# A hybrid decoder layer on one core: background steps divided by engine, more of the work turned into steps, one table for Exp and Ln

## The chip, the core and the metric

The kernel runs on one core of one Trainium2 chip. A core has a matrix engine (TensorE, PE in the profile; its weight loads are PEld), a vector engine (VectorE, DVE), an activation engine (ScalarE, ACT), GpSimd (POOL) and SyncE (SP), which only issues transfers here. Each engine works through its own instructions in their order and waits for the others by semaphores. The metric is the device time of one execution in microseconds (us), lower is better. The median of three runs before the change is 1818.29 us.

## The reference

One layer of a decoder, batch 1, 256 positions, width 2048, everything in float32:

```
h  = rmsnorm(x);  proj = h @ w_in          # 2048 columns in, 15376 out
A: gated delta rule:  q, k, v = silu(causal conv of 4 taps);  beta = sigmoid(..)
   logdecay = -exp(a_log) * softplus(.. + dt_bias);  triangular solve by chunks
   o_a = head_rmsnorm(o) * gain * silu(z_a)
B: HGRN2:  log f = logaddexp(log lb, log1p(-lb) + log_sigmoid(f));  k = -expm1(log f)
   gated linear recurrence;  o_b = head_rmsnorm(o) * gain * silu(z_b)
C: attention of 4 heads from each position into 256 memory tokens
merged = sum over A, B, C of sigmoid(gate) * (o @ w_br)
x = x + rmsnorm(merged @ w_out)
x = x + rmsnorm(relu(rmsnorm(x) @ w1)^2 @ w2)      # 8192 wide
```

All of it has to be computed; the output is x, 256 by 2048.

## The kernel before

**Units.** The large products are cut into units of 512 output columns. A unit goes through 2048 rows of weights in eight groups of 256 rows. A group's weights come in by one transfer (`w`, four buffers), ACT rounds them to `wh` (L153), DVE forms the rest `wl = w - wh` (L154), and PE multiplies by both parts: L185 to L187 in a plain unit (`unit`), L202 for the wide products and L204 for the narrow ones in a joined unit (`unit_joined`). A joined unit's result is put together from PSUM into an SBUF tile `sum` by ACT (L239) and DVE (L240). The PSUM accumulators of the units (`mm`) have two buffers, the background's banks four. Most SBUF tiles come from one pool of 25 slots (`g4`).

**Background.** Everything that isn't a unit is written as a generator: `gen_c` (attention), `gen_a` (delta rule, one for each half of the heads), `gen_b` (HGRN2, one for each half), `gen_merge` and others. A piece of a generator between two `yield`s is a *step*. The list `bg` holds the generators, and they run one after the other. After each group of a unit `tick` adds a rate to a credit and runs as many steps as the credit has whole numbers (half a group of a joined unit adds half). The rates R1 to R4 hold for the four phases: the eight units of A's projections with attention behind them; branch C (four pairs of a gate unit and a unit of `w_br`, 48 ticks); the eight units of B's projections; branch A (48 ticks), and what follows. Ahead of branch A a loop runs steps until both halves of `gen_a` are done, behind it `drain` runs whatever is left.

**Order.** The code fixes for each instruction what it depends on. A planner with its own cost table then sets the order on each engine, roughly by the order in the code among the instructions that it takes to be ready. `pin` keeps an instruction behind the one that was written before it on the same engine.

**What stands outside the steps.** `ab_unit` (beta, the log decays `ld` and their sums, with the `te` products at L660 and L661) runs as a whole ahead of A's units. `conv_evac` (the convolution: per head one ACT and three DVE operations, and one Silu), `z_evac` (Silu and a product with the gain) and `f_evac` (the forget gate: Abs, Exp, Ln, two DVE operations, four Exps) run as a whole behind their units.

**Tables.** ACT holds one set of functions at a time. The loads are put in automatically: for a function that the loaded set lacks, the first set that has it. The set found first for Exp has no Ln, so Exp, Ln, Exp takes three loads.

Lines that the prediction speaks of: L843 (X) and L849 (its transposes XT); L805 to L807 (`sse`, the power on POOL, `rq`); L790 (U and AQ); L956 (the gates' Sigmoid); L1028 and L1030 (`join_halves`); L1037 to L1051 (Exps and products of a level); L1058 (`pa` products); L1064 to L1070 (predicated copies into AT).

Of the kernel before, what the change touches and what calls it, by code (L numbers as in the profile page):

```python
# [13 lines left out]
AF = mybir.ActivationFunctionType  # L14
# [22 lines left out]
R1, R2, R3, R4 = 0.5, 1.0, 0.8, 0.8  # L37
# [3 lines left out]
def tile_trunk(ctx: ExitStack, tc, a):  # L41
# [71 lines left out]


# [328 lines left out]
    def gen_start():  # L443
# [41 lines left out]
        A.activation(e, e, AF.Exp)  # L485
# [5 lines left out]
        A.activation(lbl1, lb, AF.Ln, bias=1.0, scale=-1.0)  # L491
        c1, c2 = small("c1", 8), small("c2", 8)
        V.tensor_scalar(out=c1, in0=lb, scalar1=TINY, scalar2=None, op0=ALU.max)
        A.activation(c1, c1, AF.Ln)
# [137 lines left out]
    def ab_unit():  # L632
        wst = g4("wabs", (P, KT, 32), F32R)
        A.copy(wst[:, :, 0:16], wab)
        V.tensor_tensor(out=wst[:, :, 16:32], in0=wab, in1=wst.bitcast(F32)[:, :, 0:16], op=ALU.subtract)
        ps = bank("ab")
        for kt in range(KT):
            for i, x_ in enumerate(hact(kt)):
                T.matmul(ps[0:32, 0:S], wst[:, kt, :], x_, start=kt == 0 and i == 0, stop=kt == KT - 1 and i == 1)
        abT = g4("abT", (P, S))  # L640
        V.tensor_copy(abT[0:32, :], ps[0:32, 0:S])
        pt = bank("abt")
        for t in range(NT):
            T.transpose(pt[:, t * 32:(t + 1) * 32], abT[0:32, t * P:(t + 1) * P], ident[0:32, 0:32])
        ab2 = small("ab2", 64).rearrange("p (t c) -> p t c", t=NT)
        V.tensor_copy(ab2, pt[:, 0:64].rearrange("p (t c) -> p t c", t=NT))
        pv = small("abs", 32).rearrange("p (t c) -> p t c", t=NT)
        V.tensor_tensor(out=pv, in0=ab2[:, :, 0:16], in1=ab2[:, :, 16:32], op=ALU.add)
        A.activation(beta, pv[:, :, 0:8], AF.Sigmoid)
        xx, ax = small("xx"), small("ax")  # L650
        x3 = xx.rearrange("p (t h) -> p t h", t=NT)
        V.tensor_tensor(out=x3, in0=pv[:, :, 8:16], in1=dtb.unsqueeze(1).to_broadcast([P, NT, 8]), op=ALU.add)
        A.activation(ax, xx, AF.Abs)
        A.activation(ax, ax, AF.Exp, scale=-1.0)
        A.activation(ax, ax, AF.Ln, bias=1.0)
        V.scalar_tensor_tensor(out=xx, in0=xx, scalar=0.0, in1=ax, op0=ALU.max, op1=ALU.add)
        V.scalar_tensor_tensor(out=ld, in0=x3, scalar=-1.0, in1=alog.unsqueeze(1).to_broadcast([P, NT, 8]),
                               op0=ALU.mult, op1=ALU.mult)
        pd = bank("te")
        T.matmul(pd[:, 0:8], mgt, ld[:, 0, :], start=True, stop=True)  # L660
        T.matmul(pd[:, 8:16], caus, ld[:, 1, :], start=True, stop=True)  # L661
        A.activation(t0e, pd[:, 0:8], AF.Exp)
        A.activation(e1e, pd[:, 8:16], AF.Exp)
        V.tensor_copy(ldh, ld)
        V.tensor_tensor(out=ldl, in0=ld, in1=ldh.bitcast(F32), op=ALU.subtract)

    ab_unit()
# [6 lines left out]
    def conv_evac(ps, which, hg):  # L674
        cv = g4("cv4", (P, 4, S))
        for h in range(4):
            ct = which * 8 + hg * 4 + h
            o, p = cv[:, h, :], ps[:, h, :]
            A.activation(o, p, AF.Copy, scale=ccol[:, 72 + ct:73 + ct])
            for d in (1, 2, 3):  # L680
                tap = 3 - d
                V.scalar_tensor_tensor(out=o[:, d:], in0=p[:, 0:S - d],
                                       scalar=ccol[:, tap * 24 + ct:tap * 24 + ct + 1],
                                       in1=o[:, d:], op0=ALU.mult, op1=ALU.add)
        A.activation(cv, cv, AF.Silu)
        return cv

    def z_evac(ps, g):
        z = g4("z", (P, NT * 4, P))
        A.activation(z, ps.rearrange("p (b d) -> p b d", d=P), AF.Silu)  # L690
        V.tensor_tensor(out=z, in0=z, in1=g.unsqueeze(1).to_broadcast([P, NT * 4, P]), op=ALU.mult)
        return z
# [32 lines left out]
    def gen_a(hg, kc, qc, vc, z):  # L725
# [50 lines left out]
        for t in range(NT):  # L776
            pks = [gram(t, t, hp) for hp in range(2)]
            for h in range(4):
# [7 lines left out]
                                   op0=ALU.mult, op1=ALU.mult)  # L786
            for h in range(4):
                b = t * 4 + h
                for w, dst in ((0, U), (1, AQ)):
                    V.scalar_tensor_tensor(out=dst[:, b, :], in0=pks[h // 2][:, (h % 2) * S + w * P:(h % 2) * S + w * P + P],  # L790
                                           scalar=cneg[:, b:b + 1], in1=d2[t][:, h, w, :],
                                           op0=ALU.mult, op1=ALU.mult)
            yield
# [4 lines left out]
        for k in range(NB):  # L798
            sl = slice(k * BL, (k + 1) * BL)
            G.dma_start(scr[k].rearrange("b c m -> c b m"), U[sl, :, sl])  # L800
# [4 lines left out]
        V.tensor_scalar(out=sse, in0=sse, scalar1=EPS, scalar2=None, op0=ALU.add)  # L805
        G.tensor_tensor(out=nr, in0=sse, in1=pexp, op=ALU.pow)
        V.tensor_scalar(out=rq, in0=nr[:, 8:16], scalar1=DKS, scalar2=None, op0=ALU.mult)  # L807
# [28 lines left out]
        for c in range(BL - 2, -1, -1):  # L836
# [4 lines left out]
            if c % 2 == 0:  # L841
                yield
        V.tensor_tensor(out=X.rearrange("p b (k c) -> p b k c", c=BL), in0=Xc.unsqueeze(2).to_broadcast([P, 8, NB, BL]),  # L843
                        in1=mblk.rearrange("p (k c) -> p k c", c=BL).unsqueeze(1).to_broadcast([P, 8, NB, BL]), op=ALU.mult)
        yield
# [75 lines left out]
        yield  # L921
        yield from head_out(o, z, rq, oa, hg)

    for hg in range(2):
        kc = conv_evac(unit_joined(hboth, w_in, OFF_AK + 512 * hg), 1, hg)
        qc = conv_evac(unit_joined(hboth, w_in, OFF_AQ + 512 * hg), 0, hg)
        vc = conv_evac(unit_joined(hboth, w_in, OFF_AV + 512 * hg), 2, hg)
        z = z_evac(unit(hact, KT, w_in, OFF_AZ + 512 * hg), gna)
        bg.append(gen_a(hg, kc, qc, vc, z))
# [21 lines left out]
    def branch(gi, o, w_br):  # L951
        oact = act_of(o)
        for j in range(4):
            ps = unit(hact, KT, w_in, OFF_G + gi * D + 512 * j)
            sg = g4("sg", (P, NT, 512))
            A.activation(sg, ps.rearrange("p (t n) -> p t n", t=NT), AF.Sigmoid)  # L956
# [13 lines left out]
    def f_evac(ps, hg):  # L970
        p3 = ps
        e = g4("fe", (P, 4, S))
        A.activation(e, p3, AF.Abs)
        A.activation(e, e, AF.Exp, scale=-1.0)
        A.activation(e, e, AF.Ln, bias=1.0)
        t, g = g4("ft", (P, 4, S)), g4("fg", (P, 4, S))
        V.scalar_tensor_tensor(out=t, in0=p3, scalar=0.0, in1=e, op0=ALU.max, op1=ALU.add)
        V.scalar_tensor_tensor(out=g, in0=p3, scalar=0.0, in1=e, op0=ALU.min, op1=ALU.subtract)
        for h in range(4):
            c = hg * 4 + h  # L980
            A.activation(t[:, h, :], t[:, h, :], AF.Exp, scale=-1.0, bias=lbl1[:, c:c + 1])
        return t, g

    def gen_b(hg, k, g, q, v, z):
# [39 lines left out]
        def join_halves(s):  # L1024

            n = 1024 // (2 * s)
            pl = PP.rearrange("p h (n t s) -> p (h n) t s", t=2, s=s)
            V.tensor_tensor(out=hv(R, s, False), in0=hv(R, s, False), in1=pl[:, :, 1, s - 1:s].to_broadcast([P, n, s]),  # L1028
                            op=ALU.add)
            V.tensor_tensor(out=hv(PP, s, True), in0=hv(PP, s, True), in1=pl[:, :, 0, s - 1:s].to_broadcast([P, n, s]),  # L1030
                            op=ALU.add)
# [3 lines left out]
        for li, s in enumerate((1, 4, 16)):  # L1035
# [4 lines left out]
            V.tensor_tensor(out=seg(0, s), in0=seg(0, s), in1=bv(q, s), op=ALU.mult)  # L1040
            if s == 1:
                kp = k
            else:
                kp = kps[li % 2]
                A.activation(kp, R, AF.Exp)
                V.tensor_tensor(out=kp, in0=kp, in1=k, op=ALU.mult)
            join_halves(s)
            yield
            A.activation(seg(1, 2 * s), bv(PP, 2 * s), AF.Exp)
            V.tensor_tensor(out=seg(1, 2 * s), in0=seg(1, 2 * s), in1=bv(q, 2 * s), op=ALU.mult)  # L1050
            V.tensor_tensor(out=seg(2, 2 * s), in0=seg(1, 2 * s), in1=e1.unsqueeze(3).to_broadcast([P, 8, nb, 2 * s]),  # L1051
                            op=ALU.mult)
            join_halves(2 * s)
            yield
            pas = [bank("pa") for _ in range(4)]
            for h in range(4):
                for t in range(NT):
                    T.matmul(pas[h][:, t * 192:t * 192 + 192], kp[:, h, t * P:(t + 1) * P], qp[:, h * 2 + t, 0:192],  # L1058
                             start=True, stop=True)
            first = mT[s].bitcast(I32).rearrange("p (n r s) -> p n r s", r=4, s=s)[:, :, 1, :]  # L1060
# [11 lines left out]
            yield  # L1072

        A.activation(seg(0, 64), bv(PP, 64), AF.Exp)
        V.tensor_tensor(out=seg(0, 64), in0=seg(0, 64), in1=bv(q, 64), op=ALU.mult)
        kp = kps[1]
        A.activation(hv(kp, 64, False), hv(R, 64, False), AF.Exp)
        V.tensor_tensor(out=hv(kp, 64, False), in0=hv(kp, 64, False), in1=hv(k, 64, False), op=ALU.mult)
        join_halves(64)
        yield  # L1080
        pa = bank("pa")
# [272 lines left out]
```

## Time and profile before

| | us |
|---|---|
| median of three runs (1817.17 to 1819.19) | 1818.29 |
| the profiled execution | 1818.59 |
| its span, first to last instruction | 1816.9 |
| PE busy in the span | 1797.2 |
| DVE, ACT, POOL busy | 1133.6, 914.6, 42.9 |
| mean granted PE clock | 0.997 |

A row of a group or a wait gives the line and the engine, the tile written and the tiles read, and then times in us; a row of the order of time begins with the start from the span's beginning and the duration. A duration runs from start to end; the next instruction may start before that end. A stretch's row gives its length and each engine's busy time, then PE's granted clock (1.00 is full).

### The profile page before, as it was taken

How to read it: one execution, taken by the hardware profiler on the slowest of the kernel's cores; microseconds unless marked ns; L12 is line 12 of the kernel's file. 1: busy time of each engine (PE TensorE's matmuls, PEld its weight loads, DVE VectorE, ACT ScalarE, POOL GpSimd, SP SyncE). 2: the span in 40 equal slices, each digit the busy share in tenths (PEclk: the TensorE clock that was granted, in tenths of full speed). 3: DMA queues.
4: the chain of work that ended last, by engine and by line, in shares of the span. 5: the costliest groups of instructions: out<-in, count | busy, mean ns of one | idle time of the engine just before them, and what ended most of it. 6: DMA issues, size and time to landing. Idle time of an engine off the chain costs nothing.

```text
span 1816.9 us, 23842 instructions
## 1 busy us (share of the span) xinstructions
PE 1797.2 (99%) x9241; PEld 1533.5 (84%) x9241; DVE 1133.6 (62%) x1518; ACT 914.6 (50%) x1158; POOL 42.9 (2%) x68
## 2 busy tenths in 40 slices
PE   9999999999999989999999999999999999999998
PEld 8888888888888878888888888888888888888886
DVE  6865768746655685874555557655655565656556
ACT  6745666545546655654444445544444444444433
POOL 1100000200200000000000000000000000000000
PEclk9999999999999999999999999999999999999999
DMA  8675554855654636556766665566666676666664
GB/s 271 197 201 153 172 164 150 221 156 150 183 162 140 185 105 197 151 158 191 218 186 188 210 218 176 181 196 193 190 191 192 193 213 191 192 193 190 185 198 138
DMA packets 174946, 333.40 MB, mean 184 GB/s; under 512 B 13144, under 2 KB 14832, under 8 KB 174576
## 3 DMA queue, kind: packets, MB, share of 16 engines
q1 hardware_dynamic: 169280, 325.10, 59.6%
q10 hardware_dynamic: 4528, 4.54, 0.8%
q0 software_dynamic: 1024, 2.23, 0.7%
q8 instruction: 72, 1.18, 0.3%
q14 instruction: 42, 0.34, 0.1%
HBM read 329.60 MB, written 2.23 MB: 183 GB/s over the span
## 4 chain that ended last, share of the span: by engine, by line
PE 91%; DVE 5%; ACT 2%; issue 1%; DMA 1%; POOL 0%; DVEq 0%; POOLq 0%; ACTq 0%
PE mm L202 21%; PE mm L185 17%; PE mm L186 17%; PE mm L187 17%; PE mm L204 11%; DVE wl L154 1%; ACT wh L153 1%; DMA x<-in_x 0%; PE pzt L874 0%; PE pw L869 0%; PE pa L1058 0%; DVE AT L1067 0%; DVE bR L1028 0%; DMA w<-in_w_kv_mem 0%; DMA alog<-in_a_log 0%
## 5 line engine op out<-in xcount | busy, mean ns | idle before, releaser
L154 DVE TENSOR_TENSOR wl<-w,wh 128x1024 fp32r<-128x1024 f32 x600 | 730.3, 1222 | 533.8 <-ACT wh L153 532.9
L153 ACT CAST wh<-w 128x1024 fp32r<-128x1024 f32 x600 | 630.2, 1052 | 703.7 <-PE mm L187 444.7
L202 PE MATMUL mm<-h2h,wh 128*128 128x512 f32 x960 | 230.7, 391 | 0.0
L185 PE MATMUL mm<-wh,hh 128*128 128x512 f32 x576 | 226.4, 393 | 0.0
L186 PE MATMUL mm<-wl,hh 128*128 128x512 f32 x576 | 224.8, 390 | 1.2 <-DVE wl L154 1.2
L187 PE MATMUL mm<-wh,hh 128*128 128x512 f32 x576 | 224.8, 390 | 0.0
L202 PEld LDWEIGHTS mm<-h2h,wh 128*128 128x128 f32 x960 | 176.3, 188 | 34.0
L186 PE MATMUL mm<-wl,mh 128*128 128x512 f32 x512 | 199.2, 389 | 0.0
L185 PE MATMUL mm<-wh,mh 128*128 128x512 f32 x512 | 199.2, 389 | 0.0
L187 PE MATMUL mm<-wh,ml 128*128 128x512 f32 x512 | 199.2, 389 | 0.0
L202 PE MATMUL mm<-hh,wh 128*128 128x512 f32 x768 | 194.3, 395 | 1.0 <-DVE sum L240 1.0
L202 PEld LDWEIGHTS mm<-hh,wh 128*128 128x128 f32 x768 | 138.7, 189 | 26.1 <-DVE sum L240 1.4
L186 PEld LDWEIGHTS mm<-wl,hh 128*128 128x128 f32 x576 | 108.2, 188 | 23.2 <-DVE wl L154 1.7
L187 PEld LDWEIGHTS mm<-wh,hh 128*128 128x128 f32 x576 | 108.2, 188 | 22.5
L204 PEld LDWEIGHTS mm<-h2h,wl 128*128 128x128 f32 x960 | 123.1, 191 | 4.7
L185 PEld LDWEIGHTS mm<-wh,hh 128*128 128x128 f32 x576 | 108.2, 188 | 21.5
L204 PE MATMUL mm<-h2h,wl 128*128 128x256 f32 x960 | 124.5, 283 | 0.0
L185 PEld LDWEIGHTS mm<-wh,mh 128*128 128x128 f32 x512 | 96.1, 188 | 20.0
L186 PEld LDWEIGHTS mm<-wl,mh 128*128 128x128 f32 x512 | 96.1, 188 | 20.0
L187 PEld LDWEIGHTS mm<-wh,ml 128*128 128x128 f32 x512 | 96.1, 188 | 19.8
L204 PEld LDWEIGHTS mm<-hh,wl 128*128 128x128 f32 x768 | 103.1, 192 | 11.0 <-DVE wl L154 5.1
L204 PE MATMUL mm<-hh,wl 128*128 128x256 f32 x768 | 107.1, 285 | 4.3 <-DVE wl L154 4.3
(394 smaller groups left out, 1919.7 us busy)
## 6 DMA issues: line engine op xcount, KB each, us to landing
w<-in_w_in SPq DMA_DIRECT2D x240, 512.0 KB, 3.8
w<-in_w_mlp_in SPq DMA_DIRECT2D x128, 512.0 KB, 4.2
w<-in_w_mlp_out SPq DMA_DIRECT2D x128, 512.0 KB, 4.3
w<-in_w_out SPq DMA_DIRECT2D x32, 512.0 KB, 4.3
w<-in_w_kv_mem SPq DMA_DIRECT2D x30, 512.0 KB, 5.0
w<-in_w_br_c SPq DMA_DIRECT2D x16, 512.0 KB, 4.4
w<-in_w_br_a SPq DMA_DIRECT2D x16, 512.0 KB, 4.4
w<-in_w_br_b SPq DMA_DIRECT2D x16, 512.0 KB, 3.8
```

The lines of the kernel that those rows point to most:

```text
L153: q(A.copy(wh[:, js, 0:width], w[:, js, 0:width]))
L154: q(V.tensor_tensor(out=wl[:, js, 0:width], in0=w[:, js, 0:width], in1=wh.bitcast(F32)[:, js, 0:width], op=ALU.subtract))
L185: T.matmul(o, st, wh[:, j, :], start=kt == 0, stop=False)
L186: T.matmul(o, st, wl[:, j, :], start=False, stop=False)
L187: T.matmul(o, sl, wh[:, j, :], start=False, stop=kt == nk - 1)
L202: T.matmul(ps[c], wh[:, j, c * P:(c + 1) * P], both[j], start=k0 + j == 0, stop=end)
L204: T.matmul(ps[c][:, 0:S], wl[:, j, c * P:(c + 1) * P], both[j][:, 0:S], start=False, stop=end)
```

## The change

Six things are edited.

1. `ab_unit` becomes the generator `gen_ab` of six steps, first in the background. Its Exp follows a loaded set that has Exp and Ln both, as everywhere below where `exp_ln_table` stands: an Abs on ACT, kept behind the last Silu or Sigmoid, then the load of that set, pinned.
2. `conv_evac`, `f_evac` and the DVE part of `z_evac` become generators of five, four and one steps. `ahead_of_all` puts them at the head of `bg`, behind earlier ones of their kind.
3. `gen_a` has 44 steps instead of 41: the U and AQ copies are cut in two for each half of the positions, and an empty step stands before XT. The addition to `sse` and the power stand ahead of the second half's U and AQ, pinned; `rq` moves to the end; the first scratch DMAs are pinned.
4. `gen_b` has 42 steps instead of 20: Exps, products, the halves of `join_halves`, the `pa` products and the predicated copies (two heads at a time) are steps of their own.
5. The first Exp and Ln at the start (lower bounds) go by the joint set too.
6. The rates go from 0.5, 1.0, 0.8, 0.8 to 1.1, 1.0, 1.0, 1.2.

The core of the diff ("..." for lines left out):

```diff
-R1, R2, R3, R4 = 0.5, 1.0, 0.8, 0.8
+R1, R2, R3, R4 = 1.1, 1.0, 1.0, 1.2
...
+    def own_table(ins):
+        other_table[0] = ins.ins
+        return ins
+
+    def exp_ln_table(out, in_):
+        with tc.issue_after(other_table[0]) if other_table[0] is not None else nullcontext():
+            A.activation(out, in_, AF.Abs)
+        pin(A.preload_act_table_set("natural_log_exp_and_others"))
...
+    def ahead_of_all(gen):
+        while first_of and first_of[0] not in bg:
+            first_of.pop(0)
+        bg.insert(len(first_of), gen)
+        first_of.append(gen)
...
-    def ab_unit():
+    def gen_ab():
...
-        A.activation(ax, xx, AF.Abs)
-        A.activation(ax, ax, AF.Exp, scale=-1.0)
-        A.activation(ax, ax, AF.Ln, bias=1.0)
+        exp_ln_table(ax, xx)
+        pin(A.activation(ax, ax, AF.Exp, scale=-1.0))
+        pin(A.activation(ax, ax, AF.Ln, bias=1.0))
...
+        yield
+        yield
         pd = bank("te")
...
-    ab_unit()
+    bg.append(gen_ab())
     bg.append(gen_c())
...
-    def conv_evac(ps, which, hg):
+    def conv(ps, which, hg):
+
         cv = g4("cv4", (P, 4, S))
+        def steps():
+            for h in range(4):
...
+                yield
+            own_table(A.activation(cv, cv, AF.Silu))
+            yield
+        ahead_of_all(steps())
         return cv
...
+            if t == 1:
+                pin(V.tensor_scalar(out=sse, in0=sse, scalar1=EPS, scalar2=None, op0=ALU.add))
+                pin(G.tensor_tensor(out=nr, in0=sse, in1=pexp, op=ALU.pow))
             for h in range(4):
...
-            yield
+                if h % 2 == 1:
+                    yield
...
-            G.dma_start(scr[k].rearrange("b c m -> c b m"), U[sl, :, sl])
+            pin(G.dma_start(scr[k].rearrange("b c m -> c b m"), U[sl, :, sl]))
...
-        V.tensor_scalar(out=sse, in0=sse, scalar1=EPS, scalar2=None, op0=ALU.add)
-        G.tensor_tensor(out=nr, in0=sse, in1=pexp, op=ALU.pow)
-        V.tensor_scalar(out=rq, in0=nr[:, 8:16], scalar1=DKS, scalar2=None, op0=ALU.mult)
...
         yield
+        yield
         for t in range(NT):
             pt = bank("XT")
...
+        pin(V.tensor_scalar(out=rq, in0=nr[:, 8:16], scalar1=DKS, scalar2=None, op0=ALU.mult))
         yield from head_out(o, z, rq, oa, hg)
...
+    def forget(ps, hg):
+        t, g = g4("ft", (P, 4, S)), g4("fg", (P, 4, S))
+        def steps():
+            e = g4("fe", (P, 4, S))
+            exp_ln_table(e, ps)
+            pin(A.activation(e, e, AF.Exp, scale=-1.0))
+            pin(A.activation(e, e, AF.Ln, bias=1.0))
+            yield
+            yield
+            V.scalar_tensor_tensor(out=t, in0=ps, scalar=0.0, in1=e, op0=ALU.max, op1=ALU.add)
+            yield
+            for h in range(4):
+                c = hg * 4 + h
+                A.activation(t[:, h, :], t[:, h, :], AF.Exp, scale=-1.0, bias=lbl1[:, c:c + 1])
+            V.scalar_tensor_tensor(out=g, in0=ps, scalar=0.0, in1=e, op0=ALU.min, op1=ALU.subtract)
+            yield
+        ahead_of_all(steps())
         return t, g
...
-            V.tensor_tensor(out=seg(0, s), in0=seg(0, s), in1=bv(q, s), op=ALU.mult)
             if s == 1:
                 kp = k
             else:
                 kp = kps[li % 2]
                 A.activation(kp, R, AF.Exp)
-                V.tensor_tensor(out=kp, in0=kp, in1=k, op=ALU.mult)
-            join_halves(s)
-            yield
+            yield
+            for step in join_halves(s):
+                yield
             A.activation(seg(1, 2 * s), bv(PP, 2 * s), AF.Exp)
+            V.tensor_tensor(out=seg(0, s), in0=seg(0, s), in1=bv(q, s), op=ALU.mult)
+            yield
...
-            join_halves(2 * s)
-            yield
+            yield
+            if s > 1:
+                V.tensor_tensor(out=kp, in0=kp, in1=k, op=ALU.mult)
+                yield
             pas = [bank("pa") for _ in range(4)]
...
+            yield
             first = mT[s].bitcast(I32).rearrange("p (n r s) -> p n r s", r=4, s=s)[:, :, 1, :]
...
-            yield
+                if h % 2 == 1:
+                    yield
+            for step in join_halves(2 * s):
+                yield
```

More of the change, by code (lines that the diff above doesn't have):

```diff
@@ L1 @@
-from contextlib import ExitStack
+from contextlib import ExitStack, nullcontext
 import numpy as np
@@ L112, in tile_trunk @@
     A.copy(warm, warm)
+    other_table = [None]
+    def own_table(ins):
[5 more added lines that the diff above has]
+        pin(A.preload_act_table_set("natural_log_exp_and_others"))
     bg = []
@@ L127, in drain @@
             pump(1)
+    first_of = []
+    def ahead_of_all(gen):
[3 more added lines that the diff above has]
+        first_of.append(gen)
     rate, credit = [1.0], [0.0]
@@ L484, in gen_start @@
         V.tensor_tensor(out=e, in0=raw, in1=raw, op=ALU.subtract)
-        A.activation(e, e, AF.Exp)
+        exp_ln_table(e, e)
+        pin(A.activation(e, e, AF.Exp))
         re = small("re", 8)
@@ L490, in gen_start @@
         V.tensor_tensor(out=lb, in0=pr, in1=pr, op=ALU.subtract)
-        A.activation(lbl1, lb, AF.Ln, bias=1.0, scale=-1.0)
+        pin(A.activation(lbl1, lb, AF.Ln, bias=1.0, scale=-1.0))
         c1, c2 = small("c1", 8), small("c2", 8)
         V.tensor_scalar(out=c1, in0=lb, scalar1=TINY, scalar2=None, op0=ALU.max)
-        A.activation(c1, c1, AF.Ln)
+        pin(A.activation(c1, c1, AF.Ln))
         V.tensor_scalar(out=c2, in0=lb, scalar1=0.0, scalar2=-1e30, op0=ALU.is_le, op1=ALU.mult)
@@ L648, in ab_unit @@
         V.tensor_tensor(out=pv, in0=ab2[:, :, 0:16], in1=ab2[:, :, 16:32], op=ALU.add)
-        A.activation(beta, pv[:, :, 0:8], AF.Sigmoid)
+        own_table(A.activation(beta, pv[:, :, 0:8], AF.Sigmoid))
+        yield
         xx, ax = small("xx"), small("ax")
@@ L672, in tile_trunk @@
     ob = [None, None]
-    def conv_evac(ps, which, hg):
+    def conv(ps, which, hg):
         cv = g4("cv4", (P, 4, S))
[L676 to L685, printed above, removed]
+        def steps():
+            for h in range(4):
+                ct = which * 8 + hg * 4 + h
+                o, p = cv[:, h, :], ps[:, h, :]
+                A.activation(o, p, AF.Copy, scale=ccol[:, 72 + ct:73 + ct])
+                for d in (1, 2, 3):
+                    tap = 3 - d
+                    V.scalar_tensor_tensor(out=o[:, d:], in0=p[:, 0:S - d],
+                                           scalar=ccol[:, tap * 24 + ct:tap * 24 + ct + 1],
+                                           in1=o[:, d:], op0=ALU.mult, op1=ALU.add)
+                yield
+            own_table(A.activation(cv, cv, AF.Silu))
+            yield
+        ahead_of_all(steps())
         return cv
@@ L689, in z_evac @@
         z = g4("z", (P, NT * 4, P))
-        A.activation(z, ps.rearrange("p (b d) -> p b d", d=P), AF.Silu)
-        V.tensor_tensor(out=z, in0=z, in1=g.unsqueeze(1).to_broadcast([P, NT * 4, P]), op=ALU.mult)
+        own_table(A.activation(z, ps.rearrange("p (b d) -> p b d", d=P), AF.Silu))
+        def steps():
+            V.tensor_tensor(out=z, in0=z, in1=g.unsqueeze(1).to_broadcast([P, NT * 4, P]), op=ALU.mult)
+            yield
+        ahead_of_all(steps())
         return z
@@ L921, in gen_a @@
         yield
+        pin(V.tensor_scalar(out=rq, in0=nr[:, 8:16], scalar1=DKS, scalar2=None, op0=ALU.mult))
         yield from head_out(o, z, rq, oa, hg)
     for hg in range(2):
-        kc = conv_evac(unit_joined(hboth, w_in, OFF_AK + 512 * hg), 1, hg)
-        qc = conv_evac(unit_joined(hboth, w_in, OFF_AQ + 512 * hg), 0, hg)
-        vc = conv_evac(unit_joined(hboth, w_in, OFF_AV + 512 * hg), 2, hg)
+        kc = conv(unit_joined(hboth, w_in, OFF_AK + 512 * hg), 1, hg)
+        qc = conv(unit_joined(hboth, w_in, OFF_AQ + 512 * hg), 0, hg)
+        vc = conv(unit_joined(hboth, w_in, OFF_AV + 512 * hg), 2, hg)
         z = z_evac(unit(hact, KT, w_in, OFF_AZ + 512 * hg), gna)
@@ L955, in branch @@
             sg = g4("sg", (P, NT, 512))
-            A.activation(sg, ps.rearrange("p (t n) -> p t n", t=NT), AF.Sigmoid)
+            own_table(A.activation(sg, ps.rearrange("p (t n) -> p t n", t=NT), AF.Sigmoid))
             ps = unit(oact, 8, w_br, 512 * j).rearrange("p (t n) -> p t n", t=NT)
@@ L967, in tile_trunk, with steps @@
     branch(2, oc, a["w_br_c"][0])
[L970 to L975, printed above, removed]
-        t, g = g4("ft", (P, 4, S)), g4("fg", (P, 4, S))
[L977 to L981, printed above, removed]
+    def forget(ps, hg):
+        t, g = g4("ft", (P, 4, S)), g4("fg", (P, 4, S))
+        def steps():
+            e = g4("fe", (P, 4, S))
[11 more added lines that the diff above has]
+            yield
+        ahead_of_all(steps())
         return t, g
@@ L992, in gen_b @@
                             op0=ALU.add, op1=ALU.subtract)
-        A.activation(d, d, AF.Abs)
+            if h % 2 == 1:
+                yield
+        exp_ln_table(d, d)
+        pin(A.activation(d, d, AF.Exp, scale=-1.0))
+        pin(A.activation(d, d, AF.Ln, bias=1.0))
         yield
-        A.activation(d, d, AF.Exp, scale=-1.0)
-        A.activation(d, d, AF.Ln, bias=1.0)
         PP, R = m, g4("bR", (P, 4, S))
@@ L1045, in gen_b @@
                 A.activation(kp, R, AF.Exp)
-                V.tensor_tensor(out=kp, in0=kp, in1=k, op=ALU.mult)
-            join_halves(s)
             yield
+            for step in join_halves(s):
+                yield
             A.activation(seg(1, 2 * s), bv(PP, 2 * s), AF.Exp)
+            V.tensor_tensor(out=seg(0, s), in0=seg(0, s), in1=bv(q, s), op=ALU.mult)
+            yield
             V.tensor_tensor(out=seg(1, 2 * s), in0=seg(1, 2 * s), in1=bv(q, 2 * s), op=ALU.mult)
@@ L1052, in gen_b @@
                             op=ALU.mult)
-            join_halves(2 * s)
             yield
+            if s > 1:
+                V.tensor_tensor(out=kp, in0=kp, in1=k, op=ALU.mult)
+                yield
             pas = [bank("pa") for _ in range(4)]
@@ L1059, in gen_b @@
                              start=True, stop=True)
+            yield
             first = mT[s].bitcast(I32).rearrange("p (n r s) -> p n r s", r=4, s=s)[:, :, 1, :]
@@ L1071, in gen_b @@
                                   pa[:, :, 0, :].rearrange("p t (n s) -> p t n s", s=s))
-            yield
+                if h % 2 == 1:
+                    yield
+            for step in join_halves(2 * s):
+                yield
+        kp = kps[1]
         A.activation(seg(0, 64), bv(PP, 64), AF.Exp)
+        A.activation(hv(kp, 64, False), hv(R, 64, False), AF.Exp)
+        yield
         V.tensor_tensor(out=seg(0, 64), in0=seg(0, 64), in1=bv(q, 64), op=ALU.mult)
-        kp = kps[1]
-        A.activation(hv(kp, 64, False), hv(R, 64, False), AF.Exp)
         V.tensor_tensor(out=hv(kp, 64, False), in0=hv(kp, 64, False), in1=hv(k, 64, False), op=ALU.mult)
-        join_halves(64)
         yield
+        for step in join_halves(64):
+            pass
         pa = bank("pa")
@@ L1086, in gen_b @@
         A.copy(AT[0:64, :, 64:128], pa[0:64, :].rearrange("p (b i) -> p b i", b=8))
+        yield
         kp = kps[0]
@@ L1090, in gen_b @@
         A.activation(q3, PP[:, :, P:S], AF.Exp)
+        A.activation(kp[:, :, 0:P], R[:, :, 0:P], AF.Exp)
+        yield
         V.tensor_tensor(out=q3, in0=q3, in1=q[:, :, P:S], op=ALU.mult)
-        A.activation(kp[:, :, 0:P], R[:, :, 0:P], AF.Exp)
         V.tensor_tensor(out=kp[:, :, 0:P], in0=kp[:, :, 0:P], in1=k[:, :, 0:P], op=ALU.mult)
@@ L1114, in tile_trunk @@
     for hg in range(2):
-        k, g = f_evac(unit_joined(hboth, w_in, OFF_BF + 512 * hg), hg)
+        k, g = forget(unit_joined(hboth, w_in, OFF_BF + 512 * hg), hg)
         q = unit_joined(hboth, w_in, OFF_BQ + 512 * hg)
-        A.activation(q, q, AF.Silu)
+        own_table(A.activation(q, q, AF.Silu))
         ps = unit(hact, KT, w_in, OFF_BI + 512 * hg)
```

## The prediction

> **What bounds the kernel now.** I read the page's busy times first, then the waits of TensorE (PE), then busy time by stretch, then the order of time around each wait.
>
> ```profile
> span 1816.9 us, 23842 instructions
> PE 1797.2 (99%) x9241; PEld 1533.5 (84%) x9241; DVE 1133.6 (62%) x1518; ACT 914.6 (50%) x1158; POOL 42.9 (2%) x68
> ```
>
> The same matrix products run after the change, so PE's busy time stays and only its 19.7 us of idle time can be won. The waits say which part of it is in reach:
>
> ```profile
> PE mm L204 <- DVE wl L154: 4.3, 3, 3.1
> PE idle L310 <- POOL ident L84: 1.6, 1, 1.6
> PE te L660 <- DVE ld L657: 1.3, 1, 1.3
> PE mm L186 <- DVE wl L154: 1.2, 2, 0.7
> PE pa L1058 <- DVE qp L1051: 1.1, 1, 1.1
> PE mm L202 <- DVE sum L240: 1.0, 1, 1.0
> PE XT L849 <- DVE X L843: 0.5, 1, 0.5
> ```
>
> All but the second (the start, not touched) end on VectorE (DVE). Busy time by stretch (PE, PEld, DVE, ACT, POOL, then PE's granted clock):
>
> ```profile
> 150.00:541.00 391.00, 388.56 (x2162) 335.80 (x2161) 258.82 (x448) 216.29 (x293) 24.70 (x35) 1.00 0.59 168
> 541.00:730.00 189.00, 184.41 (x1007) 158.96 (x1006) 125.19 (x194) 111.63 (x132) 3.30 (x2) 0.99 0.53 156
> 730.00:870.00 140.00, 137.63 (x658) 115.37 (x657) 99.21 (x150) 74.67 (x81) 1.64 (x1) 1.00 0.56 168
> 870.00:1098.00 228.00, 228.00 (x1025) 188.99 (x1023) 124.28 (x115) 100.47 (x110) 0.55 (x1) 1.00 0.67 206
> 1108.00:1800.00 692.00, 692.00 (x3508) 591.99 (x3508) 407.39 (x424) 314.77 (x378) 0.00 (x0) 1.00 0.64 190
> 661.80:666.90 5.10, 1.63 (x10) 1.01 (x8) 5.10 (x7) 1.25 (x2) 0.00 (x0) 1.00 0.10 11
> 666.90:670.30 3.40, 3.23 (x12) 2.94 (x13) 3.40 (x6) 1.68 (x2) 0.00 (x0) 0.50 0.86 270
> ```
>
> PE's idle time between 150 and 870 us is 2.44 + 4.59 + 2.37 = 9.4 us, exactly the background's stages; from 870 us to the tail it is nil. Two things add to it. Right after the long wait the granted clock is 0.50 for 3.4 us, which loses 1.7 us. And a wait costs more than its idle time, since ends are modelled:
>
> ```profile
> 660.70 1.52 PE L202 MATMUL mm<-hh,wh 128*128 128x512 f32 x6
> 665.33 1.21 PE L204 MATMUL mm<-hh,wl 128*128 128x256 f32 x8 [3.12 <-DVE wl L154]
> 65.61 3.65 PE mm L202 x16
> 69.26 1.91 PE mm L204 x16
> 672.97 2.60 PE pa L1058 x16
> ```
>
> From the first of six wide products to the next product are 4.63 us; undisturbed (the last three rows are of the chain of waits) six take 6 × 3.65/16 = 1.37. The loss is 3.26 where 3.12 is counted, so I add 0.15 for each of the nine waits. **In reach: 9.4 + 1.4 + 1.7 = 12.5 us.** No gain can go beyond this except by trifles.
>
> **Why DVE is late: a budget by tick.** Each tick stands for one group of weights. In a joined unit a group is 8 wide and 8 narrow products, 8 × 0.228 + 8 × 0.119 = 2.78 us of PE; in a plain unit 12 wide ones, 2.74 us. DVE must make one wl in that time.
>
> ```profile
> 663.46 0.68 DVE L1028 TENSOR_TENSOR bR<-bR,bm 128x512 f32<-128x512 f32 x1
> 664.06 1.22 DVE L154 TENSOR_TENSOR wl<-w,wh 128x1024 fp32r<-128x1024 f32 x1
> 665.20 0.68 DVE L1030 TENSOR_TENSOR bm<-bm 128x512 f32<-128x512 f32 x1
> 658.61 0.29 DVE L1070 COPY_PREDICATED AT<-mT,pa 128x128 f32<-128x128 int32 x1
> 658.81 0.35 DVE L1067 COPY_PREDICATED AT<-mT,pa 128x64 f32<-128x64 int32 x2
> 659.07 0.29 DVE L1064 COPY_PREDICATED AT<-mT,pa 128x128 f32<-128x128 int32 x1
> ```
>
> From start to start an operation of 512 columns takes 0.60, one of 1024 columns 1.14, a predicated copy 0.20 or 0.13. So about 1.6 us of each tick are free for the background.
>
> Before, one of gen_b's levels is three steps: products and a join with kp (0.6 + 1.14 + 2 × 0.6 = 2.9), the next products with a join (4 × 0.6 = 2.4), the predicated copies (8 × 0.20 + 8 × 0.13 = 2.6): 8.0 us of DVE in three steps, 2.1 a tick at 0.8 steps a tick. With wl that is 3.2 us for a tick of 2.8, or 3.1 with the level's own products (8 × 2.60/16 = 1.3 us in three steps). DVE falls behind, and the four weight buffers hide that only for a time. The measured stretches agree:
>
> ```profile
> 750.00:770.00 20.00, 18.93 (x93) 16.23 (x92) 19.03 (x45) 13.09 (x15) 0.00 (x0) 1.00 0.51 149
> 770.00:790.00 20.00, 18.70 (x97) 15.32 (x96) 19.84 (x39) 8.68 (x11) 0.00 (x0) 1.00 0.31 92
> 817.00:862.00 45.00, 45.00 (x200) 37.25 (x200) 23.22 (x21) 17.88 (x18) 0.00 (x0) 1.00 0.64 195
> ```
>
> DVE is busy 97% of 750 to 790 us, where PE waits, and 52% once gen_b has ended. After, the level has nine steps (eight in the first), none over 1.4 us of DVE: 8.0/9 × 1.0 = 0.9 a tick in phase R3 and 1.1 in R4, with wl 2.0 and 2.2 of 2.9. The backlog that ends in a wait should not build up.
>
> **Do the steps still fit?** Counted in the code: before 16 (gen_c) + 2 × 41 (gen_a) + 2 × 20 (gen_b) = 138 steps. After: 6 (gen_ab) + 16 + 6 × 5 (conv) + 4 (z) + 2 × 44 + 2 × 4 (forget) + 2 × 42 = 236. The ticks give 64 × 1.1 + 48 + 64 + 48 × 1.2 = 240. By this count gen_a of the second half ends before branch A, as now, and gen_b's last step falls on branch A's last tick; the drain behind it finds nothing. Fifteen of the first gen_b's steps move into branch A, some 15 × 0.88 = 13 us of DVE (an estimate by the same rates: gen_b has 24 us of DVE in its levels and some 13 around them, 37 in 42 steps). With the 99.2 us of 730 to 870 that is at most 112 of 140 us there, 80%, but level.
>
> **Part by part.**
>
> A. The decays' unit becomes steps. Now PE stands for it 1.30 + 0.15. Between its producers stand three table loads, one behind the other:
>
> ```profile
> 162.53 1.28 ACT L654 ACT_TABLE_LOAD   x1
> 163.83 0.21 ACT L654 ACTIVATE ax<-ax 128x16 f32<-128x16 f32 x1
> 164.06 1.28 ACT L655 ACT_TABLE_LOAD   x1
> 166.52 1.28 ACT L662 ACT_TABLE_LOAD   x1
> ```
>
> After, one load serves both, and two yields stand before the te products. The rest of it lies beside the first A unit's products. Gain 1.4 (0 if the planner still puts te too early).
>
> B. rq leaves its place for the end of gen_a; the pow is pinned ahead of the U and AQ copies and of the scratch DMAs on POOL's queue. Now DVE stands behind the pow with eight copies and three wl queued behind it:
>
> ```profile
> 318.19 3.81 POOL L806 TENSOR_TENSOR nr<-sse,pexp 128x16 f32<-128x16 f32 x1 [226.22 <-DVE sse L805]
> 322.03 0.17 DVE L807 TENSOR_SCALAR rq<-nr 128x8 f32<-128x8 f32 x1 [2.70 <-POOL nr L806]
> 324.32 3.49 DVE L154 TENSOR_TENSOR wl<-w,wh 128x1024 fp32r<-128x1024 f32 x3
> ```
>
> PE waits there: of the 2.44 us to 541 us, te has 1.30 and XT 0.5, which leaves 0.65 for wl. Gain 0.8, with its end. The 32 scratch DMAs are the same, in the same order, and the pow runs ahead of them today too.
>
> C. The empty step ahead of XT. The wait is 0.5, but the column loop before it waits for the scratch DMAs, so the step may already lie behind the plan: I take half, 0.3.
>
> D. forget in steps, and gen_b beside it (541 to 730 us): 4.59 of idle time, 0.45 for three ends, 1.7 of clock, 6.7 in all. Now ScalarE (ACT) has a load for gen_b's Exp, then wh, kp and forget's four Exps ahead of the qp that DVE waits for:
>
> ```profile
> 655.00 1.28 ACT L1039 ACT_TABLE_LOAD   x1
> 659.27 1.70 ACT L981 ACTIVATE ft<-ft,lbl 128x256 f32<-128x256 f32 x4
> 661.52 0.69 DVE L1040 TENSOR_TENSOR qp<-qp,sum 128x512 f32<-128x512 f32 x1 [1.70 <-ACT qp L1037]
> ```
>
> After, forget goes ahead of gen_b instead of among it, with an ACT step, an empty one, a DVE one and a mixed one; its longest ACT step is 3 × 1.0 + 1.28 = 4.3 us beside two wh casts of 1.0 in two ticks of 2.8: just over, and the buffers hold it. Gain between 2 (one lump's share) and 6.7; I take 5.3, since both lumps go.
>
> E. gen_b in branch A (730 to 870 us): 2.37 of idle time and 0.45 for three ends, 2.8. DVE's load goes from 97% to some 80% at its worst, but the stretch grows. Gain 0 to 2.8; I take 1.8.
>
> F. Table loads. In the order of the steps I count 32 after, 36 now: forget, gen_b and the decays lose two each, but spreading gen_b puts branch A's four Sigmoids among its Exps, 10 loads where 6 are now. Four loads fewer are 5 us of ACT, which is half idle: nothing. Here a load takes 1.28 us and the Exp starts 0.02 later (162.53, 163.83), so the four loads more in branch A are 5.1 us, and ACT goes there from 74.7 of 140 us, 53%, to 57%. The Trainium skill (ScalarE: Activation LUTs, What ACT_TABLE_LOAD costs) puts each switch at 2.66 us with a drain, by which the four would be 10.6 us and ACT's share 61%; the sum would stay, and the trace shows no drain.
>
> G. conv and z in steps: no PE wait today ends on them, twelve conv copies a unit being hidden; they stay hidden at one head a step. The higher R4 also moves the first MLP turn one tick earlier, nearer to the relu that it waits for: 0 to one wait like te's 1.3 lost, I take 0.1, since the turn still has two groups of products ahead of it.
>
> New waits: each of gen_b's product steps now stands right behind its producer's step, and at 1.2 steps a tick every fifth tick holds two. Such a wait is 1.07 today (pa). Between 0 and 4; I take one, 1.2.
>
> **Sum:** 1.4 + 0.8 + 0.3 + 5.3 + 1.8 − 1.3 = 8.3 us. The profiled execution is 1818.59 us (span 1816.9 and 1.7 around it); the median shown is 1818.29, 0.3 lower. 1818.3 − 8.3 = **1810.0 us**.
>
> **Rivals.**
> 1. The waits only move. The planner places each engine's order by its own costs, and where PE waits is where these err; with DVE at 80% it errs elsewhere. For: only nine waits in 720 us, three of them on results the plan took as done. Against: six of the nine lie where DVE is over budget. A and B stay, D and E give 2 together, new waits 2: gain 2.2, 1816.1 us. Chance 0.18.
> 2. Slower: ACT is late at branch A's gates. Each Sigmoid of L956 then has a load before it and, when gen_b's Exp follows, one behind: 2 × 1.28 + 1.0, on top of an Exp step of up to 2 × 1.0. If wh falls four groups (11 us) behind at a gate, PE stands as at 661.8: 3.26 + 1.7 + 0.7 for a second, shorter wait = 5.6 us. It decides from two gates on: three of the four, with the gain before 730 us (7.8), give 1818.3 − 7.8 + 16.9 = 1827; two give 1821.7. Against: 57% ACT. Chance 0.09. The Trainium skill (ScalarE: Activation LUTs, Rules for kernel authors) speaks for it: finish one table set before switching, while this change scatters Exps among Sigmoids.
> 3. All of it goes, without new waits: 1818.3 − 12.5 = 1805.8. Chance 0.10.
> 4. The division has no hold: the planner already interleaves (wl stands among the predicated copies at 664 us), so steps within a tick change nothing but A and B: gain 2.2, as rival 1. Counted there.
>
> **Numbers.** Forecast 0.63 (1807 to 1814.5), rivals 0.18, 0.09, 0.10. A tell-tale difference for this kernel is 0.2%, 3.6 us. Faster: forecast, rival 3 and a little of rival 1 less the forecast's slow edge, 0.71. Same: rival 1 with that edge, 0.20. Slower 0.09. The range runs from all gained, 1805, into rival 1, 1817.5.
>
> **What would show it.** PE's idle time between 150 and 870 us near 3 us; no te wait; the clock at 1.00 throughout 541 to 730; DVE nowhere over 90% for 40 us; about 32 loads; gen_b's last transposes at the end of branch A. Wrong: waits on wl at branch A's gates, or on pa and oT, of over 4 us together, or products of the background in one lump at the drain.

## The result, and the profile after

The changed kernel takes 1807.93 us (median of six runs, 1807.24 to 1808.37), the kernel before 1818.30 (six runs): ratio 0.9942, 95% interval 0.9931 to 0.9953, or 10.4 us less. The profiled execution of the changed kernel is 1807.64 us with a span of 1805.9; 11.0 us of span are gone.

The page of the changed kernel, first lines, then all waits of PE:

```profile
span 1805.9 us, 23842 instructions
PE 1794.3 (99%) x9241; PEld 1531.7 (85%) x9241; DVE 1133.6 (63%) x1518; ACT 909.3 (50%) x1156; POOL 42.8 (2%) x68
```

```profile
PE idle L331 <- POOL ident L84: 1.6, 1, 1.6
PE dec L793 <- DVE dl L791: 1.0, 1, 1.0
PE mm L223 <- DVE sum L261: 0.3, 1, 0.3
PE pl L502 <- DMA lrow<-in_lb_raw: 0.3, 1, 0.3
```

Every one of the nine waits of before is gone: te, XT, pa, wl and sum behind gen_b. DVE's work is the same to the tenth of a microsecond (1133.6); only its place has changed. One wait is new, on dl. The same stretches as before (length, PE, PEld, DVE, ACT, POOL, clock):

```profile
150.00:541.00 391.00, 389.74 (x2145) 335.50 (x2144) 260.60 (x449) 217.68 (x295) 24.56 (x35) 1.00 0.58 169
541.00:730.00 189.00, 189.00 (x1027) 163.40 (x1026) 124.79 (x184) 105.97 (x126) 2.51 (x1) 1.00 0.56 167
730.00:870.00 140.00, 140.00 (x701) 118.60 (x701) 103.06 (x163) 77.81 (x87) 3.27 (x2) 1.00 0.55 162
760.00:780.00 20.00, 20.00 (x98) 16.87 (x97) 18.68 (x28) 14.84 (x16) 0.00 (x0) 1.00 0.59 177
780.00:800.00 20.00, 20.00 (x94) 16.99 (x93) 18.48 (x31) 10.81 (x12) 0.00 (x0) 1.00 0.54 160
```

PE's idle time between 150 and 870 us fell from 9.4 to 1.26 us, and the half clock near 667 us is gone. Over the whole span PE idles 8.1 us less (19.7 to 11.6) and is busy 2.9 us less (1797.2 to 1794.3). The last two rows are a surprise: DVE is busy 93% and 92% of these 40 us, and PE doesn't wait.

The new wait, in order of time (PE, then DVE):

```profile
278.74 1.09 PE L223 MATMUL mm<-hh,wh 128*128 128x512 f32 x4
280.79 0.47 PE L793 MATMUL dec<-dl,mgtr 128*128 128x512 f32 x1 [0.95 <-DVE dl L791]
282.04 0.93 PE L223 MATMUL mm<-hh,wh 128*128 128x512 f32 x3 [0.30 <-DVE sum L261]
```

```profile
278.81 1.22 DVE L175 TENSOR_TENSOR wl<-w,wh 128x1024 fp32r<-128x1024 f32 x1 [1.41 <-ACT wh L174]
279.96 0.69 DVE L791 TENSOR_TENSOR dl<-caus,ldh 128x512 fp32r<-128x512 f32 x1
```

DVE stood 1.41 us for a wh, and dl, which is made in the same step as the dec product that reads it, came late. With its two ends the wait costs 1.6 us.

There were 36 table loads before and are 33 now. The two largest groups are seven loads ahead of a gate's Sigmoid (four of them in branch A, three of these with a load for an Exp behind them) and six pinned loads of the joint set.

```profile
L999 ACT ACT_TABLE_LOAD x7 | 9.0, 1283 | 0.1
L124 ACT ACT_TABLE_LOAD x6 | 7.7, 1283 | 0.1
```

### The profile page after: what moved, and what is told of

It is laid out like the page before. It is cut to its first block, busy times and chain, and to the rows that moved or that the text cites. A ratio compares the mean times of both kernels' runs of the same rounds, so it can differ in the third digit from the quotient of the medians.

```text
span 1805.9 us, 23842 instructions
## 1 busy us (share of the span) xinstructions
PE 1794.3 (99%) x9241; PEld 1531.7 (85%) x9241; DVE 1133.6 (63%) x1518; ACT 909.3 (50%) x1156; POOL 42.8 (2%) x68
## 4 chain that ended last, share of the span: by engine, by line
PE 98%; issue 0%; DMA 0%; ACT 0%; DVE 0%; POOL 0%; DVEq 0%; POOLq 0%; ACTq 0%
PE mm L223 23%; PE mm L206 18%; PE mm L208 18%; PE mm L207 18%; PE mm L225 12%; PE pa L1115 1%; PE pw L911 0%; PE pzt L916 0%; DMA lrow<-in_lb_raw 0%; PE mm L367 0%; PE mm L368 0%; PE mm L370 0%; PE idle L331 0%; PE tr L1253 0%; PE tr L356 0%
```

## The experiments

Three theories stood against each other: that DVE was asked for more than a tick holds, in lumps (the prediction); that the joint table shortened ACT's chains; that the planner's order decides, whatever the steps. Every ratio is against the kernel before on the same chip, where its median was 1818.04 to 1818.30 us; two experiments set beside each other may come from different chips. The "fourth phase" of some expectations is the stage of B's projections.

**The joint table alone, on the kernel before.**

```diff
-        A.activation(e, p3, AF.Abs)
-        A.activation(e, e, AF.Exp, scale=-1.0)
+        exp_ln_table(e, p3)
+        pin(A.activation(e, e, AF.Exp, scale=-1.0))
...
```

> The kernel before with the joint set at all its places and nothing else (the Abs of gen_b stands behind its yield, so that Abs, load, Exp and Ln follow each other). Budget theory (DVE is asked for more than a tick holds, in lumps): the loads fall from 36 to about 28, but the waits on wl in 541 to 870 us stay, PE's idle time between 150 and 870 us falls from 9.4 to 6 to 9 us, mostly by the te wait; time 1814 to 1818. Rival, the table is what helped: idle time under 3 us, time 1807 to 1810.

Ratio 0.9986 (0.9977 to 0.9995), 1815.51 us, 29 loads. The te wait shrinks from 1.3 to 0.2, two loads being out of its chain. The long wait at 662 us (3.1) is gone too, but one of 1.9 us stands at 674 us in its place, with a half clock behind it, and most of the rest stays (the largest rows):

```profile
PE mm L198 <- DVE wl L166: 3.1, 3, 1.9
PE pa L1071 <- DVE qp L1064: 1.1, 1, 1.1
PE mm L214 <- DVE sum L252: 0.8, 1, 0.8
PE te L673 <- DVE ld L670: 0.2, 1, 0.2
```

PE's idle time from 150 to 870 us is still 6.9 us. So the table alone doesn't explain the gain, though by itself it is worth about 2.5 us.

**The changed kernel without the joint table.**

```diff
     def exp_ln_table(out, in_):
-        with tc.issue_after(other_table[0]) if other_table[0] is not None else nullcontext():
-            A.activation(out, in_, AF.Abs)
-        pin(A.preload_act_table_set("natural_log_exp_and_others"))
+        A.activation(out, in_, AF.Abs)
```

(and no pin on the Exps and Lns)

> The changed kernel with the loads left to be put in by function again (no preload, no pins on Exp and Ln). Budget theory: some 8 to 12 loads more, 10 to 15 us of ACT work, hidden; time 1807.5 to 1810. Rival, the table: PE waits on wl come back in 541 to 730 us, time 1812 to 1818.

1807.93 us, ratio 0.9945 (0.9931 to 0.9959), with 42 loads. Nine loads more, 11.5 us of ACT, cost nothing that can be measured. The Trainium skill (ScalarE: Activation LUTs, Rules for kernel authors) asks to finish one set before switching. Here breaking that has no price, while in the experiment before this one two loads in the chain ahead of te cost 1.1 us of waiting: what counts is where a load stands.

**Division and pace of gen_b, each alone.**

```diff
-R1, R2, R3, R4 = 1.1, 1.0, 1.0, 1.2
+R1, R2, R3, R4 = 1.1, 1.0, 1.0, 0.58     # first run: gen_b's 20 steps of before, slow
+R1, R2, R3, R4 = 1.1, 1.0, 1.0, 1.72     # second run: the 42 steps, fast
...
+        rate[0] = (R3, 0.57)[hg]             # first
+        rate[0] = (R3, 1.9)[hg]              # second
         k, g = forget(unit_joined(hboth, w_in, OFF_BF + 512 * hg), hg)
```

> The changed kernel with gen_b in the 20 steps of before, at rates that spread them as the change does (0.57 in the second half of the fourth phase's units, 0.58 in branch A). If the size of a step matters by itself: waits on wl and pa of 2 to 6 us between 600 and 870 us, time 1810 to 1814. If only the average pace matters: under 1 us of waits there, time 1807 to 1809.

> The changed kernel with gen_b's 42 steps run as fast as the 20 of before (rates 1.9 and 1.72), so that each half ends where it ended before. If pace matters (the tick's budget of DVE): DVE at 90% and more for tens of us, waits on wl and pa of 2 to 6 us, time 1810 to 1815. If division alone cures it: time 1807 to 1809.

The undivided gen_b at the new pace takes 1807.02 us (0.994, 0.9928 to 0.9952): PE is busy all of 541 to 870 us. The divided one at the old pace takes 1810.82 (0.996, 0.9948 to 0.9973), and no PE wait between 541 and 870 us is on wl either. What it has is one of its own, the output's transposes:

```profile
PE oT L760 <- DVE on L751: 2.3, 2, 1.7
```

Before the longer one DVE's product `on` itself stood 1.53 us for the power on POOL that it needs; at 1.7 steps a tick the transposes come too soon behind that chain (argued from the rate, not tried apart). So each half cures the weights' lateness alone, the division adds nothing once the pace is slow, and a full DVE by itself doesn't make PE wait. Here is the divided, fast one at the place where the kernel before waited:

```profile
760.00:780.00 20.00, 20.00 (x99) 17.44 (x98) 19.82 (x46) 9.08 (x11) 0.00 (x0) 1.00 0.59 181
```

DVE is busy 99% (98% before), and PE 100%.

**gen_b as before, steps and pace, in the changed kernel.**

```diff
-R1, R2, R3, R4 = 1.1, 1.0, 1.0, 1.2
+R1, R2, R3, R4 = 1.1, 1.0, 1.0, 0.8
...
-        (gen_b's 42 steps)
+        (its 20 steps of before)
+        rate[0] = (R3, 0.95)[hg]
```

> The changed kernel with gen_b's 20 steps of before at the pace of before (0.95 with forget's steps among them, then 0.8). The two looks before this one cured gen_b's waits by either half alone, pace or division. If gen_b undivided and fast is what made the waits: 2 to 3 us of waits on wl and pa come back in 730 to 870 us and up to 3 in 541 to 730, time 1810 to 1814. If forget and the other parts made them: under 1 us, time 1807 to 1809.

1809.82 us, 0.9956 (0.9943 to 0.9968). Two waits return, fewer than expected: the wl wait of 1.2 us after 730 us and a sum wait of 0.8 before it, 1.4 and 0.9 with their ends. (The other 0.3 of the second row stands behind dl, as in the changed kernel.)

```profile
PE mm L207 <- DVE wl L175: 1.2, 1, 1.2
PE mm L223 <- DVE sum L261: 1.1, 2, 0.8
```

The long wait near 662 us does not. Lumps and pace together make some of the waits; the long one needs something more that the change took away. forget's lump and the table loads are the candidates (the table alone moved and shortened it); no run parts them. Note the size: with gen_b left as it was, all the other edits still give 8.2 of the 10.4 us.

**forget as a lump.**

```diff
-        ahead_of_all(steps())
+        for _ in steps():
+            pass
         return t, g
```

> The changed kernel with forget's four steps run at once, right behind its unit. If the lump of the forget gate made the long wait at 661.8 us: 2 to 6 us of waits on wl or sum near 645 to 670 us, perhaps a half clock behind them, time 1810 to 1814. If gen_b's division and pace are enough: under 0.5 us there, 1807 to 1809.

1807.45 us, 0.9942 (0.993 to 0.9955); the only new wait is 0.15 us on a sum. With gen_b slow and divided, forget may be a lump. So the long wait needs an undivided, fast gen_b and something beside it.

**The pace alone, on the kernel before.**

```diff
-R1, R2, R3, R4 = 0.5, 1.0, 0.8, 0.8
+R1, R2, R3, R4 = 0.5, 1.0, 0.8, 0.57
...
+        rate[0] = (R3, 0.41)[hg]
         k, g = f_evac(unit_joined(hboth, w_in, OFF_BF + 512 * hg), hg)
```

> The kernel before with two rates changed and nothing else: 0.41 in the second half of the fourth phase's units and 0.57 in branch A, so that gen_b's 20 steps spread as the change spreads them; f_evac stays a lump. If pace alone cures what gen_b does to PE: the waits of 730 to 870 us (2.4) and most of 541 to 730 (4.6 and the half clock) go, time 1809 to 1812. If f_evac's lump makes the long wait by itself: 3 to 5 us stay near 650 to 670 us, 1813 to 1816.

1810.58 us, 0.996 (0.9948 to 0.9973): two rates give 7.7 of the change's 10.4 us. Its waits in the background's stages:

```profile
PE mm L186 <- DVE wl L154: 1.4, 2, 1.1
PE te L660 <- DVE ld L657: 1.3, 1, 1.3
PE mm L204 <- DVE wl L154: 0.7, 1, 0.7
PE XT L849 <- DVE X L843: 0.5, 1, 0.5
PE mm L202 <- DVE sum L240: 0.2, 1, 0.2
```

te, the wl at 324 us and XT are as before; of 541 to 730 us only 0.2 is left, and the clock stays whole. f_evac's lump doesn't make the long wait by itself.

**gen_ab as a lump and rq in its old place; then rq alone.**

```diff
-    bg.append(gen_ab())                  # first run only
+    for _ in gen_ab():
+        pass
...
-                pin(V.tensor_scalar(out=sse, in0=sse, scalar1=EPS, scalar2=None, op0=ALU.add))
-                pin(G.tensor_tensor(out=nr, in0=sse, in1=pexp, op=ALU.pow))
...
+        V.tensor_scalar(out=sse, in0=sse, scalar1=EPS, scalar2=None, op0=ALU.add)
+        G.tensor_tensor(out=nr, in0=sse, in1=pexp, op=ALU.pow)
+        V.tensor_scalar(out=rq, in0=nr[:, 8:16], scalar1=DKS, scalar2=None, op0=ALU.mult)
         ct0, cp0 = small("ct0", 4), small("cp0", 4)
...
-        pin(V.tensor_scalar(out=rq, in0=nr[:, 8:16], scalar1=DKS, scalar2=None, op0=ALU.mult))
```

> The changed kernel with gen_ab run at once ahead of A's units and with the addition, the power and rq where they stood before. Part A: a te wait of 0.2 to 1.5 us near 165 us (0.2 if the two loads saved were most of it, 1.3 if the missing steps were). Part B: DVE waits 2 to 3 us for rq near 320 us, and 0.5 to 0.9 us of wl wait on PE follow. Time 1808 to 1810; 1807 to 1808 if neither mattered.

> The changed kernel with the addition, the power and rq back behind the scratch DMAs, gen_ab left in steps. In the run before this one the long wl wait near 324 us came behind weight transfers of 10 us that ran beside the scratch DMAs, not behind rq, so part B is open. If the stand behind the power is what cost: DVE waits 2 to 3 us for rq near 325 us and PE waits 0.3 to 0.9 us on wl behind it, time 1808 to 1809. If not: no PE wait more than the changed kernel has, 1807 to 1808.

The first takes 1808.62 us (0.9952, 0.9939 to 0.9964): three of its five runs take 1808.2 to 1808.6 us and two 1810.1 and 1810.3. The profiled one is of the two, 1810.07 us, so its longest wait needn't be in the others. It has a te wait of 0.2 and a wl wait of 1.9 us. The long one is neither part's: rq finds its power done there, and wh stood for its weights. In order of time, ACT:

```profile
323.78 1.04 ACT L174 CAST wh<-w 128x1024 fp32r<-128x1024 f32 x1 [4.18 <-DMA w<-in_w_in]
```

then PE:

```profile
326.14 0.74 PE L225 MATMUL mm<-hh,wl 128*128 128x256 f32 x4 [1.86 <-DVE wl L175]
```

ACT stood 4.18 us for the transfer and PE 1.86 us behind it. gen_a, six steps earlier now, had sent its scratch transfers at 306 to 314 us, while the weight buffers were being refilled; in the changed kernel they go at 326 to 334 us, and the wait is missing. The second takes 1807.37 us (0.9942, 0.9929 to 0.9954): DVE waits 0.7 us for rq, twice, and PE not at all.

**conv as a lump.**

```diff
-        ahead_of_all(steps())
+        for _ in steps():
+            pass
         return cv
...
-R1, R2, R3, R4 = 1.1, 1.0, 1.0, 1.2
+R1, R2, R3, R4 = 0.63, 1.0, 1.0, 1.2
```

> The changed kernel with conv's five steps run at once behind each unit, R1 at 0.63 so that the others keep their pace. If the conv copies were hidden before (no wait ended on them): no new PE wait, perhaps the dec wait of 1.0 moves, time 1806.5 to 1808.5. If their division carried part of the gain: waits on wl or sum of 1 us and more between 170 and 350 us, 1809 to 1811.

1805.29 us, 0.993 (0.9916 to 0.9944), its five runs all below the changed kernel's six and below both ranges expected. The dec wait is gone, PE's idle time from 150 to 870 us is 0.18 us. conv in steps, together with the R1 that they need, costs the change some 2.6 us; the run doesn't part the two.

**dl one step ahead of dec, gen_b undivided and slow.**

```diff
         dec = g4("dec", (P, 8, P))
-        for t in range(NT):
+        for t in range(NT + 1):
+            if t < NT:
                 (both dl of t)
+            if t > 0:
                 (the dec products and the Exp, of t - 1)
             yield
```

> gen_b in 20 steps at the slower pace, and gen_a's dl made one step ahead of the dec products that read it (three steps instead of two), against the changed kernel's last wait, dec on dl, 1.0 us and 0.3 on sum behind it. If that wait is a product placed right behind its producer: gone, PE idle under 0.3 us between 150 and 870 us, time 1805.3 to 1806.5. If it is ACT's table load ahead of wh and sum there: it stays, 1806.8 to 1807.5.

1805.08 us, 0.9928 (0.9914 to 0.9942), the fastest of all. Its only PE wait in the whole span is the start's, and

```profile
150.00:541.00 391.00, 391.00 (x2157) 337.88 (x2157) 263.40 (x452) 216.74 (x296) 23.72 (x35) 1.00 0.56 172
541.00:730.00 189.00, 189.00 (x1038) 163.12 (x1037) 123.02 (x182) 105.34 (x125) 1.66 (x1) 1.00 0.52 163
730.00:870.00 140.00, 140.00 (x687) 118.66 (x686) 105.54 (x166) 77.61 (x85) 3.27 (x2) 1.00 0.54 171
```

PE idles nowhere from 150 to 870 us: all that the prediction called in reach is won (13.0 us against the kernel before, for 12.5). Against the undivided, slow gen_b above (1807.02 us) dl's place alone gives 1.9 us. The dec wait thus goes by two ways, dl a step ahead or conv in one piece with a lower R1; that it came of their meeting is likely, not shown.

**The few edits alone, on the kernel before.** gen_ab in steps (no joint table), the power ahead and rq at the end, the empty step ahead of XT, dl a step ahead, and gen_b's pace (0.41 and 0.57; R1 0.6, R3 0.9); conv, z, f_evac and gen_b undivided.

> The kernel before with the few edits that the looks so far found to carry the gain: gen_ab in steps, rq at the end and the power ahead, an empty step ahead of XT, dl one step ahead of dec, and gen_b's pace (0.41, 0.57); no joint table, gen_b, conv, z and f_evac undivided. If these carry it: PE idle under 1 us between 150 and 870 us, time 1805 to 1807. If the division of forget or the joint table is needed beside a slow gen_b: 2 to 5 us of waits stay in 541 to 730 us, 1808 to 1812.

1809.12 us, 0.9951 (0.9939 to 0.9964). The time fits the second branch, but the reason it gave doesn't: 541 to 730 us has 0.24 us of idle time. Two waits are left that count, the first in 730 to 870 us:

```profile
PE pa L1071 <- DVE qp L1064: 1.4, 1, 1.4
PE XT L861 <- DVE X L854: 0.7, 1, 0.7
```

The XT wait stands in spite of the empty step. Of the 4 us between this kernel and the fastest, these rows name 2.1 and their ends 0.3; the rest is open.

## Why the prediction was right, point by point

The forecast (1810.0 us, a gain of 8.3) was 2.1 us short of the 10.4 measured, within its range. The bound was right, and so was the way it was put together: 12.5 us in reach, 1.6 of it lost to a new wait, is 10.9, and the span fell by 11.0; the 1.4 and 1.7 us counted beside the idle time show up as the 2.9 us that PE is busy less. The reasons held less well than the sum, and where a size came out for another reason than the one given it was luck.

- **The tick's budget.** "The backlog that ends in a wait should not build up" came true, but the ground given, that DVE is over its budget, is too simple. By the prediction's own sum DVE was asked for about 0.1 us more than a tick holds, and at 98% of DVE in 760 to 780 us PE waits before, at 99% and 42 fast steps it doesn't. The sign "DVE nowhere over 90% for 40 us" failed; the other signs came, the idle time lower than named. What cured the lateness of the weights is an either-or: gen_b slow, or gen_b divided. For the long wait the trace before shows the step between. The wl at 664.06 us reads the first of these two wh, done near 657.5:

```profile
656.43 1.98 ACT L153 CAST wh<-w 128x1024 fp32r<-128x1024 f32 x2
```

  It stands in DVE's order behind gen_b's copies and four of its later operations, and ahead of these DVE stood idle 1.70 us for ACT's qp (the row at 661.52 in part D of the prediction), with the wl's input ready. PE began to wait near 662.2 us; a wl at 659.8 us, when DVE fell idle, would have been in time (an estimate from these starts and the wl's 1.22 us). So there it was the order, not DVE's capacity. For the other waits that is argued only.
- **D** (5.3 taken) gave all its 6.7: pace alone leaves 0.4 of it, the old gen_b beside a divided forget 0.9, the joint table alone 5.3. **E** (1.8 taken) gave all 2.8; pace alone leaves 1.7 there. Both were under-sized, and neither needs the division that the prediction gave as the ground: beside the other edits the undivided, slow gen_b leaves nothing of either.
- **A** (1.4) held; but its two causes replace each other: the lump with the joint table leaves a te wait of 0.2 (0.4 with its end), the steps without that table leave none.
- **B** (0.8): the wait went, but the mechanism isn't shown. With the power and rq back in their old place PE doesn't wait either, and DVE's wait for rq is 0.7 us instead of 2.7.
- **C** (0.3): the XT wait went, but not by the empty step alone, which leaves it at 0.7 in the last experiment.
- **F** held: 33 loads for the 32 forecast (7 from 730 to 870 us, not 10), and loads at no price beside the steps.
- **G** failed: conv's division was priced at nothing since no wait ended on conv. It cost 2.6 us together with its R1: the dec wait (1.6) and a rest that no row names.
- **New waits** (1.2): the size was near (1.6), by luck, since the place was wrong. It isn't gen_b's product steps but gen_a's dec, where producer and product share a step.
- **Rivals.** The first, that the waits only move, fell: nine went and one pair came. The slower one fell: no PE wait at any gate of branch A. The third, that all goes, missed by the dec wait. The fourth, that division changes nothing, is true of gen_b once its pace is slow; its price was wrong, since pace alone is worth 7.7 us. These worths don't add up: the other edits without gen_b's pace and division are worth 8.2.

## What to carry to other kernels

Before cutting background work finer, change its rate: where a later stage has room, spreading the same lumps over it gave three quarters of this gain by two numbers. Cut a step where a product of the full engine stands right behind its producer, and put the producer a step earlier. Once the pace was slow, finer steps in gen_b or forget brought nothing more, and those of conv, with the rate they needed, cost 2.6 us. Judge such a change by the waits of the full engine, since neither a busy feeder nor the count of table loads told where it would wait.

## What the runs showed of the hardware

**Waits of 1.9 us were followed by half the clock.** In the profiled run with gen_ab as a lump, after the 1.86 us wait (PE, PEld, DVE, ACT, POOL, clock):

```profile
324.00:327.50 3.50, 1.64 (x11) 1.31 (x10) 2.45 (x2) 2.86 (x3) 0.00 (x0) 1.00 1.03 354
327.50:330.90 3.40, 3.40 (x13) 2.92 (x12) 1.23 (x1) 1.69 (x6) 0.00 (x0) 0.50 0.86 288
```

The table alone shows the same after a wait of 1.93 us (676.6 to 680.0 us); the 1.65 us wait of the divided, fast gen_b leaves the clock at 1.00 (805 to 812 us). With the long wait before the change (3.12 us) these are the only three such stretches from 20 to 1780 us in the traces of all fourteen kernels; each lasted about 3.4 us at 0.50, 1.7 us lost. The Trainium skill (TensorE: Matmul & The Clock Gate, Why this matters for your kernels) warns of idle gaps over about 3 us; here less did it, twice.

**Beside broadcast transfers the weights came late.** In that same run the wh at 323.78 us waited for a weight transfer. The eight transfers that copy each block of the scratch to 16 partitions had been issued at 310 to 314 us. The weight transfers issued from 310 to 325 us took 10 us to land (median), those from 280 to 300 us 4.0 and those from 325 to 340 us 3.6, all of 512 KB. No run changes the broadcasts alone. A background transfer therefore has a place to be chosen too: not where the weight buffers have just run empty.
